# A hybrid layer in split float32: the residual's way through HBM, and the start of the down projection

## Chip, cores and metric

One core of a Trainium2 chip. The metric is the device time of one execution in microseconds; before the change it was 1310.67 us, the median of 3 runs (1310.51 to 1311.42).

## The reference

One layer over a residual stream x of 1024 tokens by 1024 features, float32: `x += mixer(norm(x))`, `x += cross_attention(norm(x), norm(mem))`, `x += ffn(norm(x))`, and a last norm. What the change touches stands at the last two steps:

```python
u = h @ w_up                                   # (1024, 1024) @ (1024, 5632)
u = conv_b + conv_w[0]*u[t-2] + conv_w[1]*u[t-1] + conv_w[2]*u[t]   # causal, width 3
x = x + (silu(u[:, :2816]) * u[:, 2816:]) @ w_down                  # (1024, 2816) @ (2816, 1024)
return rms_norm(x, norm_final_w)
```

## The kernel before, in words

**Arithmetic.** Each float32 operand of a large matmul is split into a rounded part `hi` and a rest `lo` (`split`, L94, and `wunit`, L109: a copy on ScalarE, ACT, and a subtraction on VectorE, DVE), and each product is three matmuls on TensorE, PE: hi·hi, hi·lo, lo·hi (`mm3c`, L909).

**Engines and order.** The code names the engine of every instruction; a scheduler at compile time orders each engine's instructions by their place in the code and by when it expects them ready. Loads and stores go through `dma` (L273), which issues on SyncE's queue (SP); GpSimd (POOL) has one load of a broadcast row ahead of each norm, and the norms' two smallest operations (L293, L294). Buffers come from pools: `big` has 40 tiles of 4 KB a partition (`f4`, `r4`), `whi` and `wlo` have 4 for split weights, `wraw` has 2 for weights as they are loaded, `tmp` has 6 (`t2`). A new tile waits until an old one of its pool is free.

**Weights of the earlier stages** come through a stream `ws` (L144): a list of units, made when a job is created with `job`; `ws.load(n)` loads and splits units up to number n, or up to the last one made, and `ws.take()` hands out the next one and loads two ahead.

**End of the attention stage (L875 to L887).** The last output projection runs tile by tile (128 tokens each). The tiles of the first half are normed and transposed; the residual x is then spilled, tile by tile, to HBM (`spill`, L796, into XS[0] to XS[7], 512 KB each). For the second half each tile, as soon as the projection has added to it, is normed (`normed`), spilled, and transposed one tile later (`HB.half1`). The code then creates the up jobs (L1166 to L1169), loads four units (L1171), lets the first products run (L1173, `fill`), and transposes the last tile (L1174).

**Up stage (`up`, L983).** 22 blocks of 128 features of each half of w_up. Each is computed for the two halves of the tokens with seven half-size products instead of eight (x, z, T2, T1, T3, B22, T4: sums and differences of input blocks), about 2.7 us of PE each. Results are copied from PSUM by ACT (`copy`, L806) or added by DVE (L803), then convolved (`conv`, L974: one ACT operation, L978, and two long DVE ones, L979 and L980), and the gated product goes to HBM as G[f]. In the last block, before the product with B22, `down_ahead(3)` (L1007) prepares three steps of the down stage.

**Down stage (`down`, L1099).** The product with w_down (2816 by 1024) is done with seven half-size products too, in passes over k = 0 to 10. Pass 1 (`units15`, L1049) loads the two G tiles and the weights of a block (1.5 MB), pass 2 (`units63`) loads more weights and keeps the G tiles, pass 3 (`units72`) likewise, and `units4` ends it. A block has two **steps**, one for each of two sets of four PSUM banks; a step is two split operands and 12 matmuls. `take` (L1093) prepares steps five ahead. Steps 0 to 21 are pass 1. The residual comes back in pass 1: after block k = 5, `residual` (L1122) takes eight tiles R of `big` and loads XS into them on SP. After pass 1, eight DVE adds put the banks onto R (`onto`, L1118); the banks X and Y keep accumulating in pass 2, after which the next adds follow, and so on to the end, where each finished tile is normed and stored.

What a step of pass 1 prepares, and the two calls around the residual:

```python
g1, g2 = a1[k], a2[k] = f4(2, TB), f4(2, TB)
dma(g1, G[k])
b11, b12 = raw_down(wd[k, :, 0, :], True)
dma(g2, G[KH + k])
yield unit(g1[:, 0, :]), unit(b11)        # step 2k
...
yield from both(X, Y, True, True, residual)   # pass 1
onto(0, lo, X)
onto(4, hi, Y)
yield from both(X, Y, False, False)           # pass 2
```

Of the kernel before, what the change touches and what calls it, by code (L numbers as in the profile page):

```python
# [17 lines left out]
D = 1024  # L18
# [5 lines left out]
NF = DFF // P  # L24
# [18 lines left out]
def hybrid_layer(ctx: ExitStack, tc: tile.TileContext, x, mem, norm_mix_w, w_in, pool_w, pool_scale,  # L43
                 gk_w2, gk_b, gla_norm_w, w_out, norm_xattn_w, norm_mem_w, wq, wkv, wo,
                 norm_ffn_w, w_up, conv_w, conv_b, w_down, norm_final_w, out):
    nc = tc.nc
# [15 lines left out]
    def nm(s):  # L62
        uid[0] += 1
        return f"{s}{uid[0]}"

    def f4(*shape):
        return big.tile([P, *shape], F32, tag="big", name=nm("f"))
# [4 lines left out]
    def t2(n=528):  # L72
        return tmp.tile([P, n], F32, tag="tmp", name=nm("t"))
# [4 lines left out]
    def bankA():  # L78
        return psA.tile([P, 512], F32, tag="psA", name=nm("pa"))

    def bankB():
        return psB.tile([P, 512], F32, tag="psB", name=nm("pb"))

    def bankU():

        turn[0] += 1
        return (bankA if turn[0] % 8 in (0, 1, 5, 6, 7) else bankB)()
# [56 lines left out]
    class Stream:  # L144
# [11 lines left out]
        def take(self, ahead=AHEAD):  # L156
            self.load(self.pos + 1 + ahead)
            w, self.units[self.pos] = self.units[self.pos], None
            self.pos += 1
            return w  # L160

    ws = Stream()
# [10 lines left out]
    def job(specs, gen):  # L173
        j = Job(specs, gen)
        for c in specs:
            ws.make.extend(c)
        plan.append(j)
        return j

    def step():  # L180

        if not plan or not plan[0].open:
            return None
        j = plan[0]
        if j.limit is not None:
            if j.limit == 0:
                return None
            j.limit -= 1
        if not hasattr(j.gen, "__next__"):
            j.gen = j.gen()  # L190
        for cost in j.gen:
            return cost
        j.done = True
        plan.pop(0)
        return 0.0

    def fill(us):
        while us > 0:
            c = step()
            if c is None:  # L200
                return
            us -= c

    def finish(j):
        while not j.done:
            plan[0].open, plan[0].limit = True, None
            step()
# [65 lines left out]
    def dma(dst, src):  # L273
        ins = nc.sync.dma_start(out=dst, in_=src)
        if starting or pinned:
            pin(ins)
# [20 lines left out]
    def normed(xt, wb, pool=None):  # L297
        y = pool.tile([P, D], F32, tag="y", name=nm("y")) if pool else f4(D)
        nc.vector.scalar_tensor_tensor(y, xt, inv_rms(xt, y), wb, ALU.mult, ALU.mult)
        return y  # L300
# [101 lines left out]
    xres = [None] * 8  # L402
# [102 lines left out]
    for xt, y in zip(mts, xn):  # L505
        rs = inv_rms(xt, y)
        for half in range(2):
            hs = slice(half * 512, (half + 1) * 512)
# [285 lines left out]
    XS = [dram.tile([P, D], F32, name=f"xd{t}", tag=f"xd{t}") for t in range(8)]  # L794

    def spill(t):  # L796
        dma(XS[t], xres[t])

    def less(dst, a, b):
        nc.vector.tensor_tensor(dst, a, b, ALU.subtract)  # L800
# [1 line left out]
    def add(dst, a, b):  # L802
        nc.vector.tensor_tensor(dst, a, b, ALU.add)  # L803

    def copy(dst, src):
        nc.scalar.activation(dst, src, AF.Copy)  # L806
# [69 lines left out]
    for t in range(4):  # L876
        spill(t)
    finish(J["wo", 1, 0])
    plan[0].open = True
    for i in range(4):  # L880
        while tiles[0] <= i:
            step()
        if i:
            HB.half1(i - 1, xn)
        xn = normed(xres[4 + i], wb_f, ybuf)
        spill(4 + i)
    finish(J["wo", 1, 512])  # L887


# [16 lines left out]
    def padd(dst, a, b):  # L906
        nc.gpsimd.tensor_tensor(dst, a, b, ALU.add)
# [7 lines left out]
    def product(ps, B, fresh):  # L915
        w = ws.take()
        for k in range(HK):
            mm3c(ps, w[:, k, :], B(k), fresh and k == 0, k == HK - 1)
            yield 0.7
# [63 lines left out]
    def up(f):  # L983
        pre = f < NPRE

        def gen():
            if pre:
                x, z = begun.pop(f)
            else:
                x = bankU()  # L990
                yield from product(x, HB["B11"], True)
            sa, ug = f4(2, TB), f4(2, TB)
            copy(sa[:, 0, :], x)
            if not pre:
                z = bankU()
                yield from product(z, HB["B21"], True)
            add(ug[:, 0, :], z, sa[:, 0, :])
            yield from product(x, HB["T2"], False)
            copy(sa[:, 1, :], x)
            y = bankB() if f in (0, 2) else bankA() if f == 1 else bankU()  # L1000
            yield from product(y, HB["T1"], True)
            sb, uv = f4(2, TB), f4(2, TB)
            copy(sb[:, 1, :], y)
            yield from product(x, HB["T3"], False)
            copy(sb[:, 0, :], x)
            padd(uv[:, 1, :], sb[:, 0, :], sb[:, 1, :])
            if f == NF - 1:  # L1007
                down_ahead(3)
            yield from product(y, HB["B22"], False)
            add(ug[:, 1, :], y, sa[:, 1, :])  # L1010
            cg = conv(ug, f)
            yield from product(x, HB["T4"], False)
            copy(uv[:, 0, :], x)
            cv = conv(uv, NF + f)
            nc.scalar.activation(cg, cg, AF.Silu)
            nc.vector.tensor_tensor(cg, cg, cv, ALU.mult)
            dma(G[f], cg)
        return job([up_units(f, "post" if pre else "all")], gen)


    R = [None] * 8
# [67 lines left out]
    def down_ahead(n):  # L1089
        while len(ready) < n:  # L1090
            ready.append(next(feed, None))
# [7 lines left out]
    def down():  # L1099
        def banks():  # L1100
            return [bankU() for _ in range(4)]

        def run(ps, fresh, stop):
            a, b = take()
            for t in range(4):
                mm3c(ps[t], a[:, t * P:(t + 1) * P], b, fresh, stop)
                yield 0.7

        def both(U, V, fu, fv, mid=None):
            for k in range(KH):  # L1110
                yield from run(U, fu and k == 0, k == KH - 1)
                yield from run(V, fv and k == 0, k == KH - 1)
                if mid and k == 5:
                    mid()

        lo, hi = slice(0, 512), slice(512, D)

        def onto(t0, hs, ps):  # L1118
            for t in range(4):
                add(R[t0 + t][:, hs], ps[t], R[t0 + t][:, hs])  # L1120

        def residual():  # L1122
            for t in range(8):
                R[t] = f4(D)
                dma(R[t], XS[t])

        X, Y = banks(), banks()
        yield from both(X, Y, True, True, residual)
        onto(0, lo, X)
        onto(4, hi, Y)  # L1130
        yield from both(X, Y, False, False)
        onto(0, hi, X)
        onto(0, hi, Y)
        turn[0] += 4
        Z = banks()
        wb = bcast_row(norm_final_w)
        yield from both(X, Z, False, True)
        onto(4, hi, X)
        onto(0, lo, Z)
        sq = [sc(2) for _ in range(4)]  # L1140
        for k in range(KH - LAST):
            yield from run(X, False, False)
            if k < 4:
                nc.sync.dma_start(out=out[k * P:(k + 1) * P, :], in_=normed(R[k], wb))
                y, r = t2(512), R[4 + k][:, hi]
                nc.scalar.activation(y, r, AF.Square, scale=1.0 / 32, accum_out=sq[k][:, 1:2])
                nc.vector.tensor_scalar(sq[k][:, 1:2], sq[k][:, 1:2], EPS, None, ALU.add)
                nc.vector.tensor_tensor(r, r, wb[:, hi], ALU.mult)
        last = [take() for _ in range(LAST)]
        for t in range(4):  # L1150
            for i, (a, b) in enumerate(last):
                mm3c(X[t], a[:, t * P:(t + 1) * P], b, False, i == LAST - 1)
                yield 0.7
            s, rs = t2(512), sc(1)
            r, rh = R[4 + t][:, lo], R[4 + t][:, hi]
            add(r, X[t], r)
            nc.scalar.activation(s, r, AF.Square, scale=1.0 / 32, accum_out=sq[t][:, 0:1])
            nc.vector.tensor_tensor(r, r, wb[:, lo], ALU.mult)
            nc.gpsimd.tensor_tensor(rs, sq[t][:, 0:1], sq[t][:, 1:2], ALU.add)
            nc.gpsimd.tensor_tensor(rs, rs, halfneg[:, 0:1], ALU.pow)  # L1160
            nc.vector.tensor_scalar(r, r, rs, None, ALU.mult)
            nc.scalar.activation(rh, rh, AF.Copy, scale=rs)
            for q, h, hs in ((nc.sync, r, lo), (nc.scalar, rh, hi)):
                q.dma_start(out=out[(4 + t) * P:(5 + t) * P, hs], in_=h)
# [3 lines left out]
    for f in range(NF):  # L1168
        up(f)  # L1169

    ws.load(ws.pos + 4)  # L1171
    plan[0].open = True
    fill(5.0)  # L1173
    HB.half1(3, xn)  # L1174
    while len(plan) > NF:
        finish(plan[0])
# [32 lines left out]
```

## Time and profile before

| | |
|---|---|
| median of 3 runs | 1310.67 us |
| the profiled execution | 1311.38 us |
| its span | 1309.4 us |
| PE busy in the span | 1271.6 us (97%) |
| DVE busy | 864.9 us (66%) |
| ACT busy | 644.8 us (49%) |
| POOL busy | 221.2 us (17%) |
| moved by DMA | 143.93 MB, mean 110 GB/s |

The span is the time between the first and the last instruction of the profiled execution. All times in rows are microseconds from the span's start. PE's row counts a matmul as busy from start to end, and matmuls overlap, so a full PE is not PE at its peak. The granted clock (PEclk) is given as a share of the full one. A released wait is put down to what came last by the profile.

### The profile page before, as it was taken

What the parts mean: (1) busy time and instruction counts of PE and PEld (TensorE: products, weight loads), DVE (VectorE), ACT (ScalarE), POOL (GpSimd) and SP (SyncE); (2) the same over time, 40 slices, a digit from 0 to 9 for tenths busy, and PEclk for the clock granted to TensorE, in tenths of its full rate; (3) what the DMA queues carried; (4) which work ended last, traced back from release to release, by engine and by line L of the source; (5) the groups of instructions that cost most, each with busy time, mean ns of one, the idle gap of its engine ahead of it and who ended that gap; (6) DMA issues with size and microseconds to landing.
All of it is one profiled execution on the core that took longest, in us unless ns stands there. A gap on an engine that the chain in (4) does not pass through costs nothing.

```text
span 1309.4 us, 16875 instructions
## 1 busy us (share of the span) xinstructions
PE 1271.6 (97%) x6326; PEld 1062.3 (81%) x6326; DVE 864.9 (66%) x1331; ACT 644.8 (49%) x1161; POOL 221.2 (17%) x230
## 2 busy tenths in 40 slices
PE   8999999999999999999899999999999999799997
PEld 7898878988788899888777888888888877578885
DVE  6723676236767554456987766776776789699765
ACT  6636534364445443335655554555555554355453
POOL 2000110001200000000034433434444410000002
PEclk9999999999999999999999999999999999899999
DMA  9333225332142122243323222222222348853202
GB/s 286 138 105 81 65 97 194 98 81 65 65 145 80 50 65 66 80 145 125 102 81 97 81 66 96 90 69 83 97 65 81 97 161 286 315 168 122 81 18 111
DMA packets 139120, 143.93 MB, mean 110 GB/s; under 512 B 4568, under 2 KB 112798, under 8 KB 139039
## 3 DMA queue, kind: packets, MB, share of 16 engines
q1 hardware_dynamic: 138031, 140.25, 33.0%
q0 software_dynamic: 432, 1.57, 0.4%
q8 instruction: 49, 0.80, 0.3%
q10 hardware_dynamic: 576, 1.05, 0.2%
q14 instruction: 32, 0.26, 0.1%
HBM read 122.93 MB, written 19.92 MB: 109 GB/s over the span
## 4 chain that ended last, share of the span: by engine, by line
PE 83%; issue 5%; DVE 5%; DMA 4%; ACT 2%; POOL 1%; SPq 0%; POOLq 0%; ACTq 0%; DVEq 0%
PE pa L90 11%; PE pa L92 11%; PE pa L91 11%; PE pa L911 9%; PE pa L912 9%; PE pa L913 9%; PE pb L911 5%; PE pb L912 5%; PE pb L913 5%; DMA f<-gd 1%; PE pb L307 1%; DVE r L97 1%; DMA wr<-in_ffn_w_up_dram 1%; DVE wl L118 1%; DVE wl L97 1%
## 5 line engine op out<-in xcount | busy, mean ns | idle before, releaser
L118 DVE TENSOR_TENSOR wl<-wr,wh 128x512 fp32r<-128x512 f32 (+1 forms) x222 | 152.9, 691 | 208.6 <-ACT wh L117 203.5
L117 ACT ACTIVATE wh<-wr 128x512 fp32r<-128x512 f32 (+1 forms) x222 | 140.0, 632 | 283.9 <-PE pa L91 82.2
L911 PE MATMUL pa<-r,wh 128*128 128x512 f32 x400 | 158.5, 396 | 7.1 <-ACT wh L117 4.6
L90 PE MATMUL pa<-wh,r 128*128 128x512 f32 (+2 forms) x480 | 159.1, 332 | 0.0
L912 PE MATMUL pa<-r,wh 128*128 128x512 f32 x400 | 158.0, 395 | 0.0
L913 PE MATMUL pa<-r,wl 128*128 128x512 f32 x400 | 157.5, 394 | 0.0
L92 PE MATMUL pa<-wh,r 128*128 128x512 f32 (+2 forms) x480 | 157.1, 327 | 0.2
L91 PE MATMUL pa<-wl,r 128*128 128x512 f32 (+2 forms) x480 | 157.2, 328 | 0.0
L90 PE MATMUL pa<-r,wh 128*128 128x512 f32 (+1 forms) x384 | 150.2, 391 | 0.7 <-ACT r L96 0.7
L92 PE MATMUL pa<-r,wl 128*128 128x512 f32 (+1 forms) x384 | 144.8, 377 | 0.3 <-DVE wl L118 0.3
L91 PE MATMUL pa<-r,wh 128*128 128x512 f32 (+1 forms) x384 | 144.7, 377 | 0.0
L92 PEld LDWEIGHTS pa<-wh,r 128*128 128x128 f32 x480 | 90.3, 188 | 9.4 <-DVE r L97 1.1
L90 PEld LDWEIGHTS pa<-wh,r 128*128 128x128 f32 x480 | 90.4, 188 | 7.8 <-ACT r L96 0.2
L91 PEld LDWEIGHTS pa<-wl,r 128*128 128x128 f32 x480 | 90.4, 188 | 7.7 <-issue 0.2
L911 PEld LDWEIGHTS pa<-r,wh 128*128 128x128 f32 x400 | 75.6, 189 | 26.0 <-ACT wh L117 4.8
L979 DVE SCALAR_TENSOR_TENSOR f<-f,vec,f 128x1023 f32<-128x1023 f32 x44 | 86.8, 1974 | 14.5 <-ACT f L978 14.5
L913 PEld LDWEIGHTS pa<-r,wl 128*128 128x128 f32 x400 | 75.5, 189 | 17.5 <-DVE wl L118 0.3
L912 PEld LDWEIGHTS pa<-r,wh 128*128 128x128 f32 x400 | 75.7, 189 | 16.7
L117 ACT ACTIVATE wh<-ws 128x512 fp32r<-128x512 f32 x88 | 55.3, 630 | 67.9 <-PE pa L912 34.0
L90 PEld LDWEIGHTS pa<-r,wh 128*128 128x128 f32 x384 | 73.2, 191 | 14.8 <-issue 1.6
L912 PE MATMUL pb<-r,wh 128*128 128x512 f32 x216 | 85.0, 393 | 0.0
L911 PE MATMUL pb<-r,wh 128*128 128x512 f32 x216 | 84.9, 393 | 0.0
(223 smaller groups left out, 2670.1 us busy)
## 6 DMA issues: line engine op xcount, KB each, us to landing
wr<-in_ffn_w_up_dram SPq DMA_DIRECT2D x47, 512.0 KB, 3.7
wr<-in_ffn_w_down_dram SPq DMA_DIRECT2D x33, 512.0 KB, 3.7
wr<-in_w_in_dram SPq DMA_DIRECT2D x24, 512.0 KB, 4.0
gd<-f SPq DMA_DIRECT2D x22, 512.0 KB, 2.6
f<-gd SPq DMA_DIRECT2D x22, 512.0 KB, 8.1
f<-in_xattn_wkv_dram SPq DMA_DIRECT2D x16, 512.0 KB, 7.6
f<-in_x_dram SPq DMA_DIRECT2D x16, 512.0 KB, 7.7
wr<-in_w_out_dram SPq DMA_DIRECT2D x16, 512.0 KB, 3.6
```

What stands on the lines that cost most here:

```text
L90: nc.tensor.matmul(ps, l.hi, r.hi, start=start, stop=False)
L91: nc.tensor.matmul(ps, l.hi, r.lo, start=False, stop=False)
L92: nc.tensor.matmul(ps, l.lo, r.hi, start=False, stop=stop)
L97: nc.vector.tensor_tensor(dst.lo, src, dst.hi.bitcast(F32), ALU.subtract)
L117: ia = nc.scalar.activation(w.hi, src, AF.Copy)
L118: ib = nc.vector.tensor_tensor(w.lo, src, w.hi.bitcast(F32), ALU.subtract)
L307: nc.tensor.transpose(ps[:, j * P:(j + 1) * P], xn[:, (4 * q + j) * P:(4 * q + j + 1) * P], ident)
L911: nc.tensor.matmul(ps, l.hi, r.hi, start=start, stop=False, **kw)
L912: nc.tensor.matmul(ps, l.hi, r.lo, start=False, stop=False, **kw)
L913: nc.tensor.matmul(ps, l.lo, r.hi, start=False, stop=stop, **kw)
L979: nc.vector.scalar_tensor_tensor(v[:, 1:], u[:, 0:T - 1], cw(1, f), v[:, 1:], ALU.mult, ALU.add)
```

## The change

1. `spill` issues its store on GpSimd's queue instead of SP's.
2. The residual isn't loaded in pass 1. The tiles R are taken after pass 1; ACT copies the banks of X and Y into one half of each. SP then loads the other half of each residual tile into the other half of R, ahead of pass 2. The half that the copies filled gets its residual in pass 3: behind each of the first eight blocks, `residual(t)` loads half a tile into a `tmp` tile and DVE adds it.
3. In the last up block, `down_ahead(4)` stands before the product with T1, instead of `down_ahead(3)` before that with B22.
4. `ws.load` is called in the loop over the last tiles, at i == 2; the call ahead of the first up products is gone, and one behind them loads up to three units ahead.

```diff
     def spill(t):
-        dma(XS[t], xres[t])
+        nc.gpsimd.dma_start(out=XS[t], in_=xres[t])
...
         spill(4 + i)
+        if i == 2:
+            ws.load(ws.pos + 4)
     finish(J["wo", 1, 512])
...
             copy(sa[:, 1, :], x)
+            if f == NF - 1:
+                down_ahead(4)
             y = bankB() if f in (0, 2) else bankA() if f == 1 else bankU()
             yield from product(y, HB["T1"], True)
...
-            if f == NF - 1:
-                down_ahead(3)
             yield from product(y, HB["B22"], False)
...
-        def both(U, V, fu, fv, mid=None):
+        def both(U, V, fu, fv, beside=None):
             for k in range(KH):
                 yield from run(U, fu and k == 0, k == KH - 1)
                 yield from run(V, fv and k == 0, k == KH - 1)
-                if mid and k == 5:
-                    mid()
+                if beside and k < 8:
+                    beside(k)
...
-        def residual():
-            for t in range(8):
-                R[t] = f4(D)
-                dma(R[t], XS[t])
+        def residual(t):
+
+            hs, r = (lo, hi)[t // 4], t2(512)
+            dma(r, XS[t][:, hs])
+            add(R[t][:, hs], R[t][:, hs], r)
 
         X, Y = banks(), banks()
-        yield from both(X, Y, True, True, residual)
-        onto(0, lo, X)
-        onto(4, hi, Y)
+        yield from both(X, Y, True, True)
+        for t in range(8):
+            R[t] = f4(D)
+        for t in range(4):
+            copy(R[t][:, lo], X[t])
+        for t in range(4):
+            copy(R[4 + t][:, hi], Y[t])
+        for t in range(8):
+            hs = (hi, lo)[t // 4]
+            dma(R[t][:, hs], XS[t][:, hs])
         yield from both(X, Y, False, False)
...
-        yield from both(X, Z, False, True)
+        yield from both(X, Z, False, True, residual)
...
-    ws.load(ws.pos + 4)
     plan[0].open = True
     fill(5.0)
+    ws.load(ws.pos + 3)
     HB.half1(3, xn)
```

## Rows read from the trace of the kernel before

**Rows 1.** Windows: stretch, its length, each engine's busy us (count), PEclk, DMA share, GB/s.

```profile
1080.00:1090.00 10.00, 8.23 (x28) 6.29 (x29) 8.77 (x14) 3.38 (x7) 0.00 (x0) 0.83 0.75 256
...
1120.00:1130.00 10.00, 2.48 (x5) 1.69 (x6) 2.96 (x5) 2.18 (x4) 0.00 (x0) 0.64 1.02 415
1130.00:1140.00 10.00, 10.00 (x39) 8.02 (x39) 9.10 (x16) 4.83 (x10) 0.00 (x0) 0.85 0.70 261
1140.00:1150.00 10.00, 8.44 (x37) 6.48 (x35) 10.00 (x17) 5.76 (x11) 0.00 (x0) 1.00 0.44 132
...
1230.00:1240.00 10.00, 10.00 (x45) 8.22 (x45) 6.91 (x11) 3.97 (x7) 0.00 (x0) 1.00 0.31 107
```

The engines of a window's row are PE, PE's weight loads, DVE, ACT and POOL, in this order.

**Rows 2.** PE's timeline in pass 1: start, us, instruction, [idle before, released by].

```profile
1119.24 0.39 PE L913 MATMUL pa<-r,r 128*128 128x512 f32 x1
1127.50 0.79 PE L911 MATMUL pb<-r,r 128*128 128x512 f32 x1 [7.87 <-ACT r L96]
...
1133.10 0.40 PE L911 MATMUL pa<-r,r 128*128 128x512 f32 x1
```

**Rows 3.** SP's timeline in pass 1.

```profile
1110.71 4.10 SPq L274 DMA_DIRECT2D f<-xd  x8
1115.35 2.36 SPq L274 DMA_DIRECT2D f<-gd  x2
```

**Rows 4.** The chain of waits in pass 1: start, us, what.

```profile
1110.71 4.58 DMA f<-xd
...
1115.35 10.93 DMA f<-gd
```

**Rows 5.** DVE's timeline in pass 1.

```profile
1126.96 0.69 DVE L97 TENSOR_TENSOR r<-f,r 128x512 fp32r<-128x512 f32 x1 [10.68 <-ACT r L96]
```

**Rows 6.** PE's timeline between pass 1 and pass 2.

```profile
1146.57 0.39 PE L913 MATMUL pa<-r,r 128*128 128x512 f32 x1
1148.52 0.47 PE L911 MATMUL pb<-r,r 128*128 128x512 f32 x1 [1.56 <-ACT wh L96]
...
1150.83 0.50 PE L911 MATMUL pb<-r,r 128*128 128x512 f32 x1 [0.68 <-DVE f L803]
```

**Rows 7.** DVE's timeline between pass 1 and pass 2.

```profile
1151.30 3.07 DVE L803 TENSOR_TENSOR f<-pa,f 128x512 f32<-128x512 f32 x5
```

**Rows 8.** PE's timeline between the up stage and pass 1.

```profile
1078.80 0.39 PE L913 MATMUL pa<-r,r 128*128 128x512 f32 x1
1081.77 2.07 PE L911 MATMUL pa<-r,r 128*128 128x512 f32 x4 [2.58 <-ACT r L96]
...
1086.24 0.85 PE L911 MATMUL pb<-r,r 128*128 128x512 f32 x3
```

**Rows 9.** DVE's timeline between the up stage and pass 1.

```profile
1075.07 2.47 DVE L979 SCALAR_TENSOR_TENSOR f<-f,vec,f 128x1023 f32<-128x1023 f32 x2
```

**Rows 10.** Groups by line and form, ACT, from 1060: count, busy, mean ns, idle before.

```profile
L806 ACT ACTIVATE f<-pa 128x512 f32<-128x512 f32 x4 | 2.4, 594 | 5.1 <-PE pa L913 5.1
```

**Rows 11.** SP's timeline at the end of the up stage.

```profile
1062.89 2.17 SPq L274 DMA_DIRECT2D f<-gd  x4
```

**Rows 12.** ACT's timeline at the end of the up stage.

```profile
1062.63 0.60 ACT L806 ACTIVATE f<-pa 128x512 f32<-128x512 f32 x1 [1.91 <-PE pa L913]
```

**Rows 13.** PE's timeline at the start of the up stage.

```profile
639.16 1.03 PE L825 MATMUL pb<-ident,y 128*128 128x128 f32 x8
644.79 0.74 PE L911 MATMUL pa<-r,wh 128*128 128x512 f32 x1 [4.60 <-ACT wh L117]
```

**Rows 14.** SP's timeline at the start of the up stage.

```profile
640.22 40.72 SPq L274 DMA_DIRECT2D wr<-in_ffn_w_up_dram  x7
```

**Rows 15.** Windows of 20 us where the residual is spilled, columns as in rows 1.

```profile
560.00:580.00 20.00, 20.00 (x151) 18.94 (x150) 9.92 (x21) 7.29 (x17) 0.63 (x1) 1.00 0.37 127
...
600.00:620.00 20.00, 19.21 (x140) 17.93 (x140) 13.56 (x25) 10.31 (x23) 1.58 (x4) 1.00 0.42 132
```

**Rows 16.** POOL's timeline where the residual is spilled.

```profile
561.03 0.63 POOL L280 DMA_DIRECT2D f<-in_norm_ffn_w_dram  x1 [154.51 <-PE pa L92]
```

**Rows 17.** DVE's timeline in pass 3.

```profile
1238.23 0.69 DVE L800 TENSOR_TENSOR wr<-f,wr 128x512 f32<-128x512 f32 x1 [1.43 <-DMA wr<-in_ffn_w_down_dram]
```

## The prediction

> **What bounds the kernel now.** I read ten-microsecond windows first, then, where TensorE (PE) is not full, its timeline, then the timelines of the queues its operands come from.
>
> The windows [rows 1] show the last stage, the three down passes, as PE's except in four places: 1080, 1120, 1130 and 1140. From 1150 on PE is full, as at 1230 (45 matmuls in 10 us, 0.222 us each). So only those holes can be won back here; work taken off DVE or ACT elsewhere is worth nothing.
>
> **The large hole** is in pass 1. PE ends step 15 at 1119.24 + 0.22 and starts step 16 at 1127.50, waiting for a split on ACT [rows 2]: 8.04 us. The next 12 matmuls take 5.60 us, to 1133.10, where 12 × 0.222 = 2.67 would do, because the granted clock has fallen (0.64 and 0.85 in those windows, between the levels 1.2 and 2.4 GHz): 2.93 us more. Together 11.0. The reason: at 1110.71 SP issues all eight residual loads (4.2 MB), and only then, at 1115.35, the activations of block k = 8 [rows 3]. By the chain of waits those take 10.93 us to land [rows 4]: DMA is at 415 GB/s in the window of 1120 [rows 1], so 4.2 MB ahead of them are 10.1 us. DVE sat idle 10.68 us behind the same split [rows 5].
>
> **Two small holes.** Between pass 1 and 2 PE stops at 1146.57, starts at 1148.52, and 6 matmuls later again only at 1150.83 [rows 6]: 1.73 + 0.98 = 2.7 us. DVE is 10.00 of 10 busy in that window [rows 1] and has the eight evacuation adds among its splits, five of them from 1151.30 in 3.07 us, 0.61 each [rows 7]. Between the up stage and pass 1 PE stops at 1078.80 + 0.22, starts at 1081.77, and takes 4.47 us for 12 matmuls [rows 8]: 2.75 + 1.80 = 4.55 us. Step 3's operands wait behind the last convolution on DVE, of which the first two operations of four take 2.47 us from 1075.07 [rows 9].
>
> **The change part by part.**
>
> *Residual out of pass 1.* The eight loads of 1110.71 go; the two loads at 1115.35 move up to 1110.7. The residual's own first load landed in 4.58 us from 1110.71 [rows 4], behind what was already under way, so they are there by 1116, and ACT and DVE need 2.5 us for the two splits. PE asks at 1119.5. So all 11.0 us go. Bounds: 6, if the next load late (the weights behind 1115.35) takes half back, to 11.0.
>
> *Evacuation after pass 1.* Eight DVE adds become eight ACT copies from PSUM, 0.594 us each [rows 10]; ACT is 5.76 of 10 busy at 1140 [rows 1]. Four copies (2.4 us) fit beside the 2.67 us of the other bank set's step, so PE should find its banks free. I take 2.4 of the 2.7 us; bounds 0 and 2.7. Eight 256 KB loads (2.1 MB, 5 us at 415 GB/s) follow on SP, ahead of pass 2's third block of weights: hidden, because steps are prepared five ahead (13 us) and the DMA share falls below a half there (0.44 at 1140 [rows 1]). If that cover were gone they'd cost those 5 us.
>
> *Eight loads and adds in pass 3.* Each add costs DVE 0.61 us [rows 7]. A block of pass 3 has six DVE operations, 3.7 us, and now 4.3, of PE's 24 × 0.222 = 5.33; the window of 1230 has DVE 6.91 of 10 busy [rows 1]. Hidden at nothing; with the cover gone 8 × 0.61 = 4.9 us. The add waits for a load, and behind it on DVE stand the splits that PE needs: that is the slower rival.
>
> *First down steps sooner, four for three.* Two products (5.3 us) earlier in the code, with four loads of g, two of weights and all ACT and DVE work of step 3 ahead of the convolution. Step 3's own wait goes; step 4 is late next, since its loads are asked for behind the convolution's tiles. Against it: buffers of a pool seem to be granted in the order the code asks. The first g loads left SP at 1062.89 [rows 11], just behind the copy at 1062.63 that first fills the tile asked for before them [rows 12]. In the new order, the up block's last tiles and weight buffers stand behind step 3's and behind the first steps' buffers, so PE will run a down step or two before the last two up products, and the convolution shifts by as much. I take 1.0 us, near nothing: the end of prepared work stays at four steps after the up stage's matmuls, and what step 4 needs stays behind the convolution. Bounds: 4.55 gained, 5 lost (two steps' worth of order that the data doesn't keep).
>
> *Weight loads at the start of the up stage.* The inserted load at i == 2 does nothing: the stream stops at the units made so far, and the up jobs are made later (L1166 to L1169). The other edit only puts the fifth unit, block 2's first, ahead of the last transposes. PE's wait there, behind the last transposes of 639.16, is 4.60 us [rows 13], for a weight load that SP can issue only at 640.22, since by the code its place is that of the tile these transposes read [rows 14]. Neither edit frees it sooner. I take 0; bounds 0 and 4.6.
>
> *Spills on GpSimd's queue.* SP loses eight issues and their waits for the residual's adds. PE stands idle 0.79 us in the window of 600 to 620 and not at all in the others from 560 to 640 [rows 15], so at most 0.8 us can come of it. GpSimd's one load there took 0.63 us of the engine [rows 16]; a spill ahead of a norm's two small operations delays that norm by this, beside a full PE. Value 0; bounds 0.8 gained, 8 × 0.63 = 5 lost. The Trainium skill, page "SBUF — State Buffer", section "SBUF: two separate sides", warns that a DMA issued by GpSimd cannot write its descriptors while VectorE holds the port the two share, and gives 3.1 us in place of 0.62. By that, as an estimate, each of the four norms with a spill ahead of it could come 2.5 us later than by the row, 10 us in all with nothing hidden, and the sum would be 4.4; no row of before shows such a store. "DMA: Bandwidth & Descriptors", section "Issuing engines are not separate DMA queues", says that more issuing queues only save issue time; by that the move gives 0 and not 0.8.
>
> **Sum:** 11.0 + 2.4 + 1.0 = 14.4 us. The profiled execution took 1311.38 us (span 1309.4), 0.71 over the median of 1310.67. 1311.38 − 14.4 = 1297.0, and against the median 1296.3.
>
> **The rivals.**
> 1. *The sooner steps hurt.* PE waits at the end of the up stage for weight buffers that down steps hold. For: the order in [rows 11, 12]. Against: the four steps keep PE supplied meanwhile. 5 lost in place of 1.0 gained: 1302.3. Chance 0.15.
> 2. *Pass 1 is still short of data.* For: DVE and DMA are busy all through it, and weights follow the activations on SP. Against: 1.5 MB a block at 415 GB/s is 3.8 us of 5.33. Half of the 11.0 stays: 1301.8. Chance 0.10.
> 3. *The up stage's start gains too*, because SP is freed: 4.6 more, 1291.7. Against: its wait is for a place, not for SP. Chance 0.06.
> 4. *Slower: DVE waits for the residual in pass 3.* Each of eight adds stands on DVE until a load just issued lands. DVE already waited 1.43 us for a weight load at 1238.23 [rows 17]. The spare time is 5.33 − 4.3 = 1.0 us a block. At the 4.58 us of the residual's load in the chain [rows 4] it loses 8 × 3.6 = 29 us, less some 10 for the steps prepared ahead: 1296.3 + 19 = 1315. It decides from (14.4 + 10)/8 + 1.0 = 4 us a load. Against: the loads can be issued a block ahead. Chance 0.04.
> 5. *The residual's loads land as early as before*, since the buffers are free and SP runs ahead: the hole stays, and the rest evens out at 1310.7. Chance 0.03; the tiles are asked for after the last step of pass 1.
>
> **How the numbers follow.** The forecast has the other 0.62, with 1292.4 to 1300.7 of its own: 11.0 + 2.7 + 4.55 at most, and 11.0 with nothing for the evacuation and 1.0 lost at the first steps. The range takes in rivals 1 to 3, 1291.7 to 1302.3, with a microsecond or two for the room in the other terms: 1290 to 1303.5. A measurement of this kernel can tell 0.2%, 2.6 us: faster 0.62 + 0.15 + 0.10 + 0.06 = 0.93; same 0.03; slower 0.04.
>
> **What would show it.** Right: no residual load on SP before step 21; PE full from step 4 to the end of pass 1; eight ACT copies from PSUM at its end without a PE gap of over 0.3 us; no DVE wait of over 1 us at a residual add in pass 3; PE's wait at the up stage's start still near 4.6 us. Wrong: a PE gap of some microseconds inside pass 1, the last two up products behind down steps with gaps between, or a norm late on GpSimd.

## The result, and the profile after

The changed kernel took **1302.14 us** (median of four runs, 1301.40 to 1303.83), the kernel before 1311.0 beside it (four runs): ratio 0.9934, 95% interval 0.9917 to 0.9952. A second set of five runs, made later beside the experiments, gave 1300.52, ratio 0.9915 (0.9902 to 0.9929). The forecast was 1296.3 with a range of 1290 to 1303.5: the sign and the range held, but each beside its own runs of the kernel before, the two sets gained 8.9 and 11.2 us of the 14.4.

To see where, I subtracted the start of the n-th matmul in the trace after from that of the n-th in the trace before (both have 6326), at the stage borders. Positive is gained. The times are those of the trace before, and "start" is all up to 577, where no edit reaches. There, all traces of this document lie between −0.6 and +1.2, so this much is what one execution differs from another by.

```
stage (us, trace before)     start   577-676  676-697  697-1056  1056-1103  1103-1143  1143-1160  rest    all
forecast                      0        0        0         0        +1.0      +11.0       +2.4      0    +14.4
after, first profile         +0.7     -2.1     -2.1       0        -0.95     +10.9       +2.4     +0.2   +9.1
after, second profile        +0.8     -2.1      0         0        -0.1      +10.9       +1.4     +0.2  +11.05
```

So pass 1 came as forecast, the evacuation in part, and the first steps not; and the stretch from 577 to 676 lost what no term had. In the windows of the last stage, columns as in [rows 1], the holes at 1120 and 1130 are gone, and most of that at 1140; what is left is the one at 1080, behind which the granted clock fell for a while (0.83 in the window of 1090, a mean between the levels 1.2 and 2.4 GHz):

```profile
1080.00:1090.00 10.00, 7.33 (x31) 5.27 (x30) 9.30 (x11) 4.24 (x6) 0.00 (x0) 1.00 0.44 175
1090.00:1100.00 10.00, 9.74 (x36) 7.44 (x35) 6.88 (x12) 4.50 (x8) 0.00 (x0) 0.83 0.82 305
...
1120.00:1130.00 10.00, 10.00 (x46) 8.28 (x45) 8.75 (x15) 4.86 (x9) 0.00 (x0) 1.00 0.90 348
1130.00:1140.00 10.00, 10.00 (x45) 8.19 (x44) 10.00 (x17) 5.29 (x11) 0.00 (x0) 1.00 0.63 202
1140.00:1150.00 10.00, 9.88 (x43) 7.78 (x43) 9.11 (x16) 9.63 (x20) 0.00 (x0) 1.00 1.01 364
```

SP's timeline in pass 1 of the kernel after answers to [rows 3]. Activations and weights follow one another with nothing between them, and the residual's first loads leave at 1136.31, when PE is at pass 1's last step but one (the forecast had them not before the last):

```profile
1115.50 0.86 SPq L274 DMA_DIRECT2D f<-gd  x2
1119.89 0.33 SPq L274 DMA_DIRECT2D wr<-in_ffn_w_down_dram  x1
1120.28 2.07 SPq L274 DMA_DIRECT2D f<-gd  x4
...
1136.31 2.27 SPq L274 DMA_DIRECT2D f<-xd  x5
...
1140.05 1.97 SPq L274 DMA_DIRECT2D f<-xd  x3
```

The evacuation, on ACT's timeline: eight copies from PSUM in two groups.

```profile
1139.93 1.55 ACT L806 ACTIVATE f<-pb 128x512 f32<-128x512 f32 x3
1141.36 0.60 ACT L806 ACTIVATE f<-pa 128x512 f32<-128x512 f32 x1
...
1143.92 2.07 ACT L806 ACTIVATE f<-pa 128x512 f32<-128x512 f32 x4
```

On PE's timeline the first matmul of pass 2 starts 0.51 us behind the one before it (0.222 is the usual step), where [rows 6] had gaps of 1.56 and 0.68:

```profile
1140.04 0.39 PE L915 MATMUL pa<-r,r 128*128 128x512 f32 x1
1140.55 0.50 PE L913 MATMUL pb<-r,r 128*128 128x512 f32 x1
```

In pass 3 the residual's loads leave SP from 1178.56 and their eight adds run from 1187.6 to 1215.2; none of them stands in the list of what DVE waited for, in which only weight loads and ACT's splits appear. The group of these adds:

```profile
L803 DVE TENSOR_TENSOR f<-f,t x8: 677/682/686, 1187.6 to 1215.2; 128x512 f32<-128x512 f32 x8
```

**What I had not seen coming** is on GpSimd's timeline. It answers to [rows 16]: the load of the norm's weight row, which left at 561.03 before, now stands behind two spills, and these wait for the projection's last add (DVE L435, which ends at 578.6):

```profile
577.67 1.17 POOL L797 DMA_DIRECT2D xd<-f  x2 [171.91 <-DVE f L435]
578.82 0.55 POOL L280 DMA_DIRECT2D f<-in_norm_ffn_w_dram  x1
```

The row needs 8.0 us to land, and on DVE's timeline the first norm waits 4.51 us for it. First its row before, without a wait, then after:

```profile
583.04 1.28 DVE L299 SCALAR_TENSOR_TENSOR f<-f,s,f 128x1024 f32<-128x1024 f32 x1
```

```profile
586.93 1.28 DVE L299 SCALAR_TENSOR_TENSOR f<-f,s,f 128x1024 f32<-128x1024 f32 x1 [4.51 <-DMA f<-in_norm_ffn_w_dram]
```

On PE's timeline the transposes behind that norm wait. Later PE waits 0.29 and 0.34 us, at 609.67 and 610.40, for the two halves of a weight split, and 1.04 us for a weight split that it had waited 0.79 us for before, which was then all of its wait in this stretch ([rows 15]). The rows after:

```profile
588.27 1.09 PE L825 MATMUL pb<-ident,f 128*128 128x128 f32 x8 [0.47 <-DVE f L299]
...
614.45 0.39 PE L90 MATMUL pa<-r,r 128*128 128x256 f32 x1 [1.04 <-ACT r L117]
```

and before:

```profile
613.07 0.39 PE L90 MATMUL pa<-r,r 128*128 128x256 f32 x1 [0.79 <-ACT r L117]
```

From the up stage to pass 1, PE's timeline answers to [rows 8]. 28 matmuls of the first down steps run from 1068.58 on, ahead of the last 24 of the up stage, which go from 1075.26 to 1080.91 (at 1080.91 the down steps go on). The wait of 2.58 us at the start of step 3 is gone, and 0.67 and 2.00 us stand in its place: a split of ACT (L96) and one of DVE (L97) were queued behind the convolution and the gate that follows it.

```profile
1068.58 0.39 PE L913 MATMUL pb<-wh,wh 128*128 128x512 f32 x1
...
1075.26 0.50 PE L913 MATMUL pa<-r,wh 128*128 128x512 f32 x1
...
1080.91 0.39 PE L913 MATMUL pa<-wh,wh 128*128 128x512 f32 x1
...
1086.37 0.97 PE L913 MATMUL pb<-r,r 128*128 128x512 f32 x3 [0.67 <-ACT r L96]
...
1089.57 0.50 PE L914 MATMUL pb<-r,r 128*128 128x512 f32 x1 [2.00 <-DVE r L97]
```

At the up stage's start, nothing changed against [rows 13]: the transposes end and PE waits 4.45 us.

```profile
646.04 0.51 PE L913 MATMUL pa<-r,wh 128*128 128x512 f32 x1 [4.45 <-ACT wh L117]
```

### The profile page after: what moved, and what is told of

It is laid out like the page before. It is cut to its first block, busy times and chain, and to the rows that moved or that the text cites. A ratio compares the mean times of both kernels' runs of the same rounds, so it can differ in the third digit from the quotient of the medians.

```text
span 1300.4 us, 16897 instructions
## 1 busy us (share of the span) xinstructions
PE 1269.9 (98%) x6326; PEld 1059.7 (81%) x6326; DVE 862.9 (66%) x1331; ACT 648.7 (50%) x1169; POOL 227.7 (18%) x238
## 4 chain that ended last, share of the span: by engine, by line
PE 67%; issue 16%; DVE 7%; DMA 4%; ACT 3%; POOL 1%; SPq 0%; POOLq 0%; ACTq 0%; DVEq 0%
PE pa L913 8%; PE pa L914 8%; PE pa L915 8%; PE pa L92 8%; PE pa L90 8%; PE pa L91 8%; PE pb L913 5%; PE pb L914 5%; PE pb L915 5%; DVE r L97 2%; DMA f<-gd 2%; DVE wl L118 1%; PE pb L307 1%; DMA f<-in_norm_ffn_w_dram 1%; DVE wl L97 1%
## 5 line engine op out<-in xcount | busy, mean ns | idle before, releaser
L913 PEld LDWEIGHTS pa<-r,wh 128*128 128x128 f32 x400 | 75.9, 190 | 26.5 <-ACT wh L117 4.7
L914 PEld LDWEIGHTS pa<-r,wh 128*128 128x128 f32 x400 | 75.9, 190 | 17.0
L915 PE MATMUL pb<-r,wl 128*128 128x512 f32 x216 | 84.7, 392 | 0.0
```

Source lines behind the costliest of these rows:

```text
L913: nc.tensor.matmul(ps, l.hi, r.hi, start=start, stop=False, **kw)
L914: nc.tensor.matmul(ps, l.hi, r.lo, start=False, stop=False, **kw)
L915: nc.tensor.matmul(ps, l.lo, r.hi, start=False, stop=stop, **kw)
```

## The experiments

In the edits, - is the kernel named first and + the experiment. The stage differences are made as in the table above, each against the same trace of before.

**Spills back on SP.**

```
-        nc.gpsimd.dma_start(out=XS[t], in_=xres[t])
+        dma(XS[t], xres[t])
```

> The changed kernel with one line as before: the eight spills issued by SP. Theory A: on GpSimd's queue the first two spills stand ahead of the load of the norm's weight row and wait for the last projection's adds; the row, and with it the first norms, come late, and PE loses 2.1 us from 577 to 613. With the spills on SP the row leaves GpSimd near 561 again, PE starts the up stage's first matmuls 2.1 us sooner, and the time is 1302.1 - 2.1 = 1300.0. Theory B: the row was not what PE waited for, or other work takes the place: 1302.1, and the row early with the loss still there. Open beside it: whether the loss of 2.1 us from 691 to 697 (PE waiting 1.8 us for a split on ACT, then half the clock) goes too; if it hangs on the order that the spills leave, 1298.

Measured: 1299.0 us, ratio 0.9897 (0.9881 to 0.9912). The row leaves GpSimd at 561.53, the first norm starts at 583.55, and the difference from 577 to 676 is −0.3 in place of −2.1. GpSimd's timeline:

```profile
561.53 0.63 POOL L280 DMA_DIRECT2D f<-in_norm_ffn_w_dram  x1 [154.53 <-PE pa L92]
```

Theory A. The loss from 676 to 697 was not there either, but it was in no trace except the changed kernel's first, so it says nothing on the spills.

**The row by SP, the spills left on GpSimd.**

```
-    wb_f = bcast_row(norm_ffn_w)
+    wb_f = bcast_row(norm_ffn_w, nc.sync)
```

> The changed kernel with the spills still on GpSimd, but the load of the norm's weight row issued by SP. Theory A (the row stands behind two spills that wait): the row lands early, the norm starts as before the change, 2.1 us come back: 1300.0. Theory B (the spills themselves slow GpSimd's small norm operations, each by 0.6 us of issue or by 2.5 us of waiting for a port): the row is early but the second to fourth norm are still late on GpSimd, the loss stays: 1302.1.

Measured: 1301.66 us (0.9907 to 0.9932), −3.3 us from 577 to 676. Neither theory had this: on SP's timeline the row is late too, behind six weight loads that wait for their buffers until 580.8, and it is there at 589.19 for DVE, later than in the changed kernel:

```profile
544.98 35.85 SPq L274 DMA_DIRECT2D wr<-in_xattn_wo_dram  x6
580.89 0.48 SPq L280 DMA_DIRECT2D f<-in_norm_ffn_w_dram  x1
```

The condition (an early row) was not made, so the run doesn't tell A from B; it shows the same cost by another queue, and more of it: PE waits 1.89 us for the first norm in place of 0.47.

**The weight loads at the up stage's start as before.**

```
-        if i == 2:
-            ws.load(ws.pos + 4)
...
+    ws.load(ws.pos + 4)
     plan[0].open = True
     fill(5.0)
-    ws.load(ws.pos + 3)
```

> The changed kernel with the weight loads at the start of the up stage as before: nothing loaded at i == 2, four units asked for ahead of the fill, none behind it. Theory: neither edit frees the place that the loads wait for, PE's wait at the up stage's start stays at 4.5 us, the time at 1302.1. Rival: the edit changes the order in which the buffers of the up stage's first units are asked for, and with it the 2.1 us lost from 691 to 697: 1300.0.

Measured: 1300.95 us (0.9900 to 0.9927), PE's wait 4.57 us. The edits are worth nothing that these runs can tell.

**The down steps as late as before.**

```
-            if f == NF - 1:
-                down_ahead(4)
             y = bankB() if f in (0, 2) else bankA() if f == 1 else bankU()
...
+            if f == NF - 1:
+                down_ahead(3)
             yield from product(y, HB["B22"], False)
```

> The changed kernel with three down steps prepared ahead of the B22 product, as before, in place of four ahead of the T1 product. Theory A (the sooner steps put down steps ahead of the last two up products, whose splits and convolution then come late): the gaps of 0.7 and 2.0 us at 1086 to 1090 go, the wait of 2.6 us at the start of pass 1 returns with its time at half the clock; together 0.95 us better, 1301.2. Theory B (the sooner steps are worth the 1.0 us predicted): 1303.1. In pass 1 nothing changes by either.

Measured: 1300.32 us (0.9897 to 0.9924). The total is below both theories' and doesn't tell them apart. As both have it, the wait of 2.58 us is back on PE's timeline, and the gaps at 1086 to 1090 are gone:

```profile
1083.97 1.46 PE L913 MATMUL pa<-r,r 128*128 128x512 f32 x4 [2.58 <-ACT r L96]
1085.73 0.80 PE L914 MATMUL pa<-r,r 128*128 128x512 f32 x1 [0.30 <-DVE r L97]
```

The difference from 1056 to 1103 is −0.1, against −0.95 and −0.1 in the two profiles of the changed kernel and −0.3, −0.2 and −0.1 in the three runs above, which have the sooner steps. So the 0.95 that theory A went by is not what the sooner steps cost each time, and B's gain isn't there either.

**The spills alone, in the kernel before.**

```
-        dma(XS[t], xres[t])
+        nc.gpsimd.dma_start(out=XS[t], in_=xres[t])
```

> The kernel before with one line changed: the eight spills on GpSimd's queue. By the runs so far, the spills stand ahead of the weight row's load on that queue whatever the down passes do. Theory A: the row leaves GpSimd near 579 in place of 561, lands near 587, the first norm ends 3.5 to 4 us later than before, PE falls 1.6 to 2.1 us behind from 577 to 613, and the rest of the kernel is as before: 2 us slower, 1313.5 beside 1311.5. Theory B (the loss hangs on something else that the changed kernel has there): same time, no loss from 577 to 613.

Measured: 1313.38 us beside 1311.84, ratio 1.0013 (1.0005 to 1.0021): 1.5 us slower, and −2.3 from 577 to 676. GpSimd's timeline is that of the changed kernel, and so is the norm's on DVE's, below it:

```profile
577.40 1.16 POOL L797 DMA_DIRECT2D xd<-f  x2 [171.85 <-DVE f L435]
578.55 0.54 POOL L280 DMA_DIRECT2D f<-in_norm_ffn_w_dram  x1
```

```profile
586.87 1.28 DVE L299 SCALAR_TENSOR_TENSOR f<-f,s,f 128x1024 f32<-128x1024 f32 x1 [4.71 <-DMA f<-in_norm_ffn_w_dram]
```

Theory A, alone and without the rest of the change.

**The order of the code kept on GpSimd's queue: row, norms, spills.** Row and spills are held in program order.

```
-        nc.gpsimd.dma_start(out=XS[t], in_=xres[t])
+        pin(nc.gpsimd.dma_start(out=XS[t], in_=xres[t]))
...
-        if starting:
+        if starting or src is norm_ffn_w:
             pin(ins)
```

> The changed kernel with the order on GpSimd's queue kept as the code has it: the weight row's load first, then the spills, still on that queue. Issuing the row from SP left it late too, since SP was then held by a weight load that waited for its buffer until 580.9. Theory A (the place behind the waiting spills is the whole cost): the row leaves near 561, the first norm comes near 583, the loss from 577 to 613 goes, 1302.1 - 2.1 = 1300.0 or the 1299.0 of the kernel with its spills on SP. Theory B (a spill on GpSimd costs the norms beside it too): part of the loss stays, over 0.5 us from 577 to 613.

Measured: 1304.68 us (0.9932 to 0.9956), slower than the changed kernel. The row is early and the stretch from 577 to 600 loses nothing, as A has it. But the four first spills now leave as one burst at 601.46, DMA is full from 605 to 610, the weights of the output projection take 7.3 us to land (median; 3.6 before), PE waits 2.79 us and runs at a lower clock until 620 (0.94 and 0.72). GpSimd's timeline:

```profile
561.29 0.63 POOL L280 DMA_DIRECT2D f<-in_norm_ffn_w_dram  x1 [154.51 <-PE pa L92]
...
601.46 2.21 POOL L797 DMA_DIRECT2D xd<-f  x4
```

The windows, columns as in [rows 1], and below them PE's timeline:

```profile
605.00:610.00 5.00, 4.68 (x34) 4.18 (x32) 3.06 (x5) 1.28 (x3) 0.00 (x0) 1.00 1.01 340
610.00:615.00 5.00, 2.19 (x13) 1.99 (x14) 2.55 (x6) 2.49 (x6) 0.00 (x0) 0.94 0.17 46
615.00:620.00 5.00, 5.00 (x33) 4.99 (x33) 2.51 (x7) 2.55 (x6) 0.00 (x0) 0.72 0.62 188
```

```profile
612.47 0.38 PE L90 MATMUL pa<-wh,r 128*128 128x256 f32 x1 [2.79 <-ACT wh L117]
```

By number, over 0.5 us lost by 613 (4.0), this is B; by mechanism it is not, since the norms are on time (the first at 583.31). The same transfers cost 6.1 us from 577 to 676 here, for a reason that neither theory had.

**Row, then the four spills, then the norms.** As the last one, and the first four spills stand ahead of the norms in the code.

```
-    weave(norm0(HB, wb_f))
     for t in range(4):
         spill(t)
+    weave(norm0(HB, wb_f))
```

> The changed kernel with GpSimd's queue in this fixed order: the weight row's load, the first four spills right behind it, then the norms. Theory A (a spill on GpSimd's queue costs nothing where it stands neither ahead of the row nor, as four at once near 601, ahead of the weights of the next product): the row leaves near 561, the four spills near 578 to 580, no loss over 0.3 us from 577 to 640, 1299 to 1300. Theory B (a spill on GpSimd's queue has a cost of its own for the norms behind it): over 1 us is still lost there, 1301 or more.

Measured: 1300.36 us (0.9900 to 0.9927), nothing lost from 577 to 600, −2.0 from 577 to 676. The row leaves at 560.55 and the spills run from 577.88 to 579.98. But DVE's timeline has the first norm at 588.00, though by then its row and its scale (GpSimd, 582.4) are long there: in this program two weight splits that wait for ACT were put ahead of it.

```profile
584.58 0.69 DVE L118 TENSOR_TENSOR wl<-wr,wh 128x512 fp32r<-128x512 f32 x1 [1.95 <-ACT wh L117]
587.39 0.69 DVE L118 TENSOR_TENSOR wl<-wr,wh 128x512 fp32r<-128x512 f32 x1 [2.11 <-ACT wh L117]
588.00 1.28 DVE L299 SCALAR_TENSOR_TENSOR f<-f,s,f 128x1024 f32<-128x1024 f32 x1
```

From 577 to 640 this program lost 0.7 us, between A's 0.3 and B's 1, so A's version was not made cleanly, and whether a spill on GpSimd has a small cost of its own beside its place is left open. Two things can be read all the same. GpSimd stood idle again, waiting for ACT, ahead of the norm's operation behind those four spills (1.53 us), so the spills didn't hold that norm up there. And a late first norm isn't a loss in itself: this one is later than in the changed kernel, but PE's order has its transposes nine matmuls further back (589.95), and PE doesn't wait for them.

**The residual loaded in pass 1, but spread.** In the kernel before, one load behind each of the blocks 2 to 9.

```
-                if mid and k == 5:
-                    mid()
+                if mid and 2 <= k < 10:
+                    mid(k - 2)
```

(and the function behind it loads the one tile that it is given)

> The kernel before, with the residual still loaded in pass 1, but one of the eight 512 KB loads behind each of the blocks 2 to 9 in place of all eight behind block 5. Nothing else is changed. Theory A (the hole comes of eight loads in one burst ahead of the next block's activations): DMA has 1.5 + 0.5 = 2.0 MB a block, 4.8 us at 415 GB/s beside PE's 5.3, so PE stays supplied and 8 to 11 us come back, some 1302. Theory B (pass 1 has no room for 4.2 MB more, in whatever order): the wait is spread over the blocks, and less than half of it, under 5 us, comes back: over 1306.

Measured: 1306.87 us (0.9949 to 0.9974), 5.0 less than before: B's total. By place it is half of each: pass 1 gives back 9.0 of the 10.9, and the stretch from 1143 to 1160 takes 4.3 away again. The windows (columns as in [rows 1]) show DMA full at 1120 while DVE has 7.36 of 10, so the splits fall behind, and DVE, with the eight evacuation adds in its queue, full from 1130 on:

```profile
1120.00:1130.00 10.00, 8.93 (x40) 7.06 (x39) 7.36 (x13) 3.52 (x7) 0.00 (x0) 1.00 1.00 394
1130.00:1140.00 10.00, 8.38 (x37) 6.32 (x35) 9.96 (x17) 4.84 (x9) 0.00 (x0) 1.00 0.81 257
1140.00:1150.00 10.00, 7.21 (x21) 5.61 (x22) 10.00 (x18) 3.34 (x7) 0.00 (x0) 0.66 0.61 205
```

On PE's timeline the step that follows waits 4.40 us for a split:

```profile
1142.79 0.76 PE L911 MATMUL pb<-r,r 128*128 128x512 f32 x1 [4.40 <-ACT wh L96]
```

The burst made the large hole; spread, the same bytes still leave pass 1 without a reserve at its end.

**The evacuation on DVE, in the changed kernel.**

```
-            copy(R[t][:, lo], X[t])
+            nc.vector.tensor_scalar(R[t][:, lo], X[t], 1.0, None, ALU.mult)
```

(and the same for the four tiles of Y)

> The changed kernel with the eight evacuations of pass 1's banks on DVE (a multiply by 1.0 from PSUM to SBUF) in place of ACT's eight copies. Theory A (the 2.35 us gained between pass 1 and 2 come from DVE freed of those eight operations): the two gaps of PE at the start of pass 2 come back, about 2 us, 1304 in place of 1302. Theory B (they come from the supply, which is further ahead once the residual's burst is gone from pass 1): the gaps stay away, 1302, within 0.5 us.

Measured: 1306.27 us (0.9944 to 0.9968), −1.0 from 1143 to 1160 in place of +2.4 and +1.4. Theory A by the trace, though the median is 2.3 us above A's 1304 (the traced execution took 1304.49): the gaps are back, 2.3 and 0.9 us on PE's timeline, the second behind DVE's evacuation itself:

```profile
1141.60 0.47 PE L913 MATMUL pb<-r,r 128*128 128x512 f32 x1 [2.29 <-ACT wh L96]
1143.91 0.50 PE L913 MATMUL pb<-r,r 128*128 128x512 f32 x1 [0.91 <-DVE f L1135]
```

**The changed kernel once more.**

> The changed kernel itself, run and profiled once more. In its first profile PE lost 2.1 us from 691 to 697 behind a split on ACT; seven profiles of kernels that have the same program there did not show it, and its sooner down steps lost 0.95 us against 0.1 to 0.4 in three others. Theory A (both are what one execution does and another doesn't): no loss from 691 to 697, 0.0 to 0.4 us lost at the first steps, the loss of 1.6 to 2.1 us from 577 to 613 there again; 1300.5 to 1302. Theory B (they belong to this program): both again, 1302.1 and more.

Measured: 1300.52 us. Theory A. The wait for ACT near 691 is there in both traces, 1.28 us in this one and 1.24 to 1.29 in all others, but 1.85 in the first; and only in the first did the granted clock fall behind it. So 0.6 of the 2.1 us is the longer wait, and 1.5 the clock. The execution that was traced first took 1303.83 us, the longest of its four; whether the other three lost the same, no trace shows. Windows of the first profile, and in the second block of the second:

```profile
690.00:695.00 5.00, 3.15 (x13) 2.21 (x12) 4.59 (x4) 4.58 (x7) 2.58 (x2) 0.94 0.35 100
695.00:700.00 5.00, 5.00 (x18) 3.97 (x17) 5.00 (x6) 1.70 (x4) 1.88 (x1) 0.72 0.03 7
```

```profile
690.00:695.00 5.00, 3.72 (x17) 2.72 (x16) 5.00 (x5) 4.47 (x7) 3.17 (x2) 1.00 0.24 69
695.00:700.00 5.00, 5.00 (x23) 3.90 (x22) 4.62 (x6) 1.71 (x4) 1.20 (x1) 1.00 0.15 43
```

It also shows the evacuation's other end: here PE waits 1.17 us for an ACT copy, so this term was 1.4 and not 2.4. ACT's order is the same in both traces: the copies stand behind splits, and the first of these waits 3.14 us for DVE. What differs is where PE stands. Here its last matmul of pass 1 is done at 1137.07 + 0.22, 0.7 us ahead of the first copy; in the first profile it was done 0.3 us behind that copy's start (1139.93). ACT's row and then PE's:

```profile
1138.00 1.55 ACT L806 ACTIVATE f<-pb 128x512 f32<-128x512 f32 x3
```

```profile
1138.63 0.50 PE L913 MATMUL pb<-r,r 128*128 128x512 f32 x1 [1.17 <-ACT f L806]
```

**Spills on SP and late steps; and the residual's way alone.** The first is the changed kernel with the edits of the first and fourth experiment, the second has the third's too, so that only the residual's way and its evacuation are left of the change.

> The changed kernel with its spills on SP and three down steps prepared late as before, so that of the change the residual's way, the evacuation by ACT and the weight loads at the up stage's start are left. Against the kernel with only its spills on SP (1299.0) this shows the sooner steps alone. Theory A (sooner steps cost some tenths): 1298.7, PE's wait of 2.6 us at the start of pass 1 there in place of the gaps at 1086 to 1090. Theory B (they are worth the 1.0 us predicted): 1300.

> The kernel before with the residual's way and the evacuation by ACT alone: spills on SP, steps and weight loads as before. Theory (all of the gain is in these two): 1311.8 - 10.9 - 2.4 = 1298.5, and no loss from 577 to 613. Rival (the other edits carry part of it): 1300 or more.

Measured: 1298.34 us (0.9887 to 0.9914) and 1299.57 us (0.9891 to 0.9918). The first is near A's 1298.7; the second lies between its theory's 1298.5 and its rival's 1300, and no slower than the changed kernel, so no gain is missing without the other edits. All of it is in the residual's way with its evacuation: pass 1 gave 10.8 in both, the evacuation 2.8 and 1.0. The first-steps term came out at −1.9 in the one and +0.15 in the other, with the same late steps and the same wait of 2.58 us (the first has 0.57 us of wait more behind it), so A's total in the first run is no proof of A's mechanism.

## Why the prediction was right, and where it was wrong

The range held in part by luck. The forecast's own bounds, 1292.4 to 1300.7, hold the second set (1300.52) and not the first (1302.14), and the wider range took that in only because of rivals 1 and 2, neither of which came at its price. What was lost was lost in terms put at nothing or near it. Of the named signs, a residual load left ahead of step 21 and PE had a gap of 1.17 us behind pass 1 in the second profile; and two signs of being wrong were there, down steps ahead of the last up products with gaps behind them, and a late norm.

**Residual out of pass 1: right.** 11.0 forecast, 10.5 to 10.9 in the eleven traces that have this edit. With the loads spread the hole went too, but not the price: only half came back.

**Evacuation: right in kind, and its size depends on where PE stands.** 2.4 forecast; 1.0 to 2.8 in ten traces with ACT's copies, −1.0 with DVE's. The step "PE should find its banks free" counted ACT's busy share and not what stands ahead of a copy on ACT.

**Loads and adds in pass 3: right.** No wait, no cost. The slower rival's condition never came up.

**Weight loads at the up stage's start: right** at nothing (4.45 and 4.57 us of wait with and without).

**First down steps sooner: wrong by 1.0.** The step that failed is "Step 3's own wait goes". It went, and rival 1's mechanism put 2.3 to 2.7 us of gaps in its place (two profiles), as its condition said (down steps ahead of the last up products), at a price near nothing and not 5. In eight traces with the sooner steps the stretch gave −1.2 to +0.2, mean −0.4; in the five without, −1.9 to +0.2, mean −0.5.

**Spills on GpSimd's queue: wrong by some 2 us, and this is the step that cost most.** "Value 0" went through what a spill does ahead of a norm's two small operations (0.63 us, hidden), and not through what else is issued on that queue, though [rows 16] showed it: the weight row. Nor did I ask what a spill waits for; its issue is short, but it holds the queue from 561 to 577.67. The bound "8 × 0.63 = 5 lost" held the size by chance: the delay that it counts is not in the rows (in the second half, behind each spill of 0.62 us, GpSimd still waited 0.41 us for ACT before the norm's first operation). With spills on SP the stretch from 577 to 676 lost 0.2 to 1.0 us (four traces), with the order of the change 2.1 to 2.8 (six). Up to 640 alone the two are further apart: 0.0 to 0.1 against 1.7 to 2.2. By runs: 1.5 us alone; three kernels with spills on SP have medians of 1298.3 to 1299.6, the changed kernel and the two that differ from it only in steps or weight loads 1300.3 to 1302.1.

On the port, the delay estimated from the Trainium skill's page "SBUF — State Buffer", section "SBUF: two separate sides", did not come: single spills took 0.58 to 0.63 us of GpSimd and four in a row 2.21, 0.55 each, in a window with DVE 3.57 of 5 busy; 3.1 us is seen nowhere. The page's own case is a VectorE operation in a two-port mode, such as a float32 copy within SBUF; beside the spills DVE ran tensor_tensor and scalar_tensor_tensor operations only, so no run here shows that copy beside a spill. The Trainium skill's page "DMA: Bandwidth & Descriptors", section "Issuing engines are not separate DMA queues", agrees with the trace in that, with SP rid of eight issues, nothing came sooner.

**The sum**, against the second profile: 14.4 − 2.1 (spills) − 1.1 (first steps) − 1.0 (evacuation) − 0.1 (pass 1), and + 0.8 ahead of 577 and + 0.2 behind 1160, for which nothing was forecast, is 11.1; measured 11.05. The 2.1 put down to the spills has some tenths in it that kernels with their spills on SP lose too. The first profile lost another 2.1 from 676 to 697.

## What to carry to other kernels

A DMA moved to another engine's queue is not priced by its issue time: list all that is issued on that queue near it, and ask what the moved one waits for, since everything behind it waits too. After that, look at the built order on every queue, for it need not be that of the code. Where a hole is closed, ask which engine used it to catch up; here, with the hole closed and the evacuation left to DVE, the next gap grew by 1.0 us in place of shrinking by 1.0 to 2.8.

## What the runs showed that I had not expected

A wait can cost its length or its length and a stretch of lower clock: behind the wait near 691 the windows show 1.00 in one execution (1.28 us of wait) and 0.94 and 0.72 in another (1.85 us), 2.1 us apart; behind the unchanged wait of 2.58 us at step 3 the stretch came out between −1.9 (with a second wait of 0.57 us) and +0.2. So one profile of a kernel of this kind can't settle a term under 2 us; it took several kernels that share the stretch.

The row's load took 4.9 us to land where it left ahead of the spills [rows 16] and 8.0 behind two of them on the same queue. The spills' own landing doesn't go by the queue: their medians are 3.0 to 4.9 us in the kernels that issue them on GpSimd and 3.5 to 4.8 in those on SP.
